# A hybrid RWKV-7 and delta-net layer on one core: scans of two head pairs in one list of steps, decays from running sums read in rows, overlapped inversions, spread modulation sums

## The chip, the cores and the metric

The kernel runs on one core of one Trainium2 chip. The metric is the time of one execution on the device, in microseconds (us), as the median of three runs. A profile of one execution tells where the time goes; its engines are PE (TensorE matmul), PEld (TensorE's weight loads), DVE (VectorE), ACT (ScalarE), POOL (GpSimd) and SP (SyncE, which here only issues DMAs).

## What is computed

One layer over 256 latent tokens and 256 context tokens, 2048 channels, all in float32. The tokens are normalised and modulated, projected once, and go through two token mixers; these are merged, and a feed-forward block follows. Cut to what matters here:

```python
h  = modulate(rmsnorm(x, norm1_w), sh1, sc1)         # x (1, 256, 2048); hc the same of ctx
rw, cv, z, ab, gt = split(h @ w_in, IN_SPLITS)       # and of hc
# RWKV-7: 16 heads of 64, both directions, context first, its final state starts the latents
def step(s, inp):
    r_t, w_t, k_t, v_t, kk_t, b_t = inp
    sa = einsum('bhij,bhj->bhi', s, kk_t)
    s = s * w_t[:, :, None, :] - sa[..., None] * b_t[:, :, None, :] + v_t[..., None] * k_t[:, :, None, :]
    return s, einsum('bhij,bhj->bhi', s, r_t)
# gated delta-net: 8 heads of 128, both directions, chunked
gc    = cumsum(chunks(g), axis=-1)
diff  = gc[..., :, None] - gc[..., None, :]
decay = where(incl, exp(where(incl, diff, 0.0)), 0.0)
lmat  = where(strict, einsum('nbhik,nbhjk->nbhij', kb, kc) * decay, 0.0)
sol   = triangular_solve(lmat, rhs, lower=True, unit_diagonal=True)
q_dec, k_tail, g_last = qc * exp(gc), kc * exp(gc[-1:] - gc), exp(gc[-1])
# merge, output projection, then
x = x + gt1 * y
x = x + gt2 * swiglu(modulate(rmsnorm(x, norm2_w), sh2, sc2), w_gate_up, w_down)
return rmsnorm(x, final_norm_w)
```

## The kernel before

Three stages follow each other. The first makes the modulation of the first norm and the low-rank columns of the projection. The second, some 1125 us long, is written with a planner of its own and is where the change lies. The third runs the merge, the output projection and the feed-forward block as a plain stream of large matmuls.

Every large product is split: a weight `w` is cast to a rounded high part (`whi`, on ACT) and a rest (`wlo`, on DVE), the activations likewise (`hxh`, `hxl`), and three matmuls `hxh,whi`, `hxl,whi`, `hxh,wlo` are added up (line 145 in the second stage, since each operation is recorded through one helper; lines 370 to 372 in the others). A product of 16 weight tiles is thus 48 matmuls of 128x512 (context and latents) or 128x256 (latents alone).

In the second stage each part of the work is a generator that yields operations: `prepare(p)`, `grams(p, d)`, `inverse(p)`, `values(p)`, `scan(p)` for the eight RWKV head pairs p, and `features(h)`, `tokens(h)`, `decays(h)`, `head_grams(h)`, `head_inverse(h)`, `head_scan(h)` for the eight delta-net heads h; `products()` makes all projections, of which 40 gate columns ("g") can be made at nearly any time; `ada_rest()` sums up modulation columns on DVE. The class `Weave` holds a clock for each engine and repeatedly takes the operation that could start first, with the rank of its generator as the tie-break. Its estimates are the numbers of `LAT`: `hop` for the way from one engine to another, `own` for the way to the next operation on the same engine, `turn` for a switch of PE between tile shapes, `grp` for the most matmuls that are issued before it chooses again. It runs when the program is built; what it leaves is a fixed order of instructions for each engine, which then waits on semaphores alone. A generator can also wait for a name that another one has declared ready ("scan", p).

The parts that the change touches:

- `scan(p)` runs the two directions of one pair through eight steps, four over the context (n < 4) and four over the latents. A step is a chain: four small matmuls into a PSUM bank (`s<-VX,LAc` or `s<-VX,LAl`), a copy on ACT (`R`), four matmuls with the inverse (`s<-R,Tx`), two copies on ACT (`VX`), four matmuls with the keys (`s<-VX,KB`), two multiplications on DVE (`VX<-s,et`). Pair p waits for pair p-1.
- `decays(h)` makes for each direction the matrix exp(gc_i - gc_j). It multiplies a triangle of ones by the gates on DVE (`gm`), sums over the tokens in between by a 128x512 float32 matmul with the constant `aft`, takes the exponential on ACT, and masks the result on POOL. A second float32 matmul, 128x256 with `ones`, gives the exponent for the queries (`Qe`).
- `invert(...)` inverts the triangular blocks. Its substitution works on 16x16 blocks that go through DRAM (`scr`, `tscr`) on SP's queue; `head_inverse(h)` starts when that of head h-1 is complete.
- `ada_rest()` loads 64 tiles of 128x1024 on POOL's queue and adds each, times a scalar, to a sum on DVE (`aw<-aw,ck`, two instructions a tile). It starts when the RWKV part is done and goes on as fast as its buffers allow.

Of the kernel before, what the change touches and what calls it, by code (L numbers as in the profile page):

```python
# [11 lines left out]
F32 = mybir.dt.float32  # L12
# [6 lines left out]
P = 128  # L19
D = 2048  # L20
KT = D // P
T = 256
# [7 lines left out]
LAT = dict(dma=2.4, hop=0.3, own=0.1, grp=32, crank=-1, cg=4, turn=0.13)  # L30
# [7 lines left out]
for _name, _w in (("ident", 128), ("ones", 128), ("bd64", 128), ("rmask", 256),  # L38
                  ("low16", 2), ("eye16", 32), ("tri", 256), ("aft", 256), ("q4", 4), ("q2", 2),
                  ("eps", 1), ("gneps", 1)):  # L40
    _C[_name] = (_n, _n + _w)
    _n += _w
# [12 lines left out]
def const_array():  # L55
# [19 lines left out]
    put("aft", np.concatenate([u > v, u < v], 1))  # L75
# [195 lines left out]
def emit(ctx: ExitStack, tc, A, out, dbg=None):  # L271
# [37 lines left out]
    aft = c_("aft").rearrange("p (d t) -> p d t", d=2)  # L309
# [219 lines left out]
    def shift(ps, M, j, dst, ctx_part=True):  # L529

        n = 512 if ctx_part else T
# [11 lines left out]
        if ctx_part:  # L543
            yield add(dst[:M, T + 1:512], ps[:M, T:511], mc[:M, j, 0:1])
            yield add(dst[:M, T:511], ps[:M, T + 1:512], mc[:M, j, 1:2])
# [10 lines left out]
    def invert(pool, Lt, parts, nu, which, full, fill):  # L556
# [11 lines left out]
        Tx = pool.tile([P, nu, 64], F32, tag="ivx", name="Tx", bufs=2)  # L568
# [25 lines left out]
        yield dq(blocks(tl, nb), TT[:nb], 2)  # L594
        for h in range(2):
# [16 lines left out]
        Qm = xt[:, :16 * nu].rearrange("p (u c) -> p u c", c=16)  # L612
# [39 lines left out]
        if full:  # L652
# [3 lines left out]
            for h in range(2):  # L656
# [9 lines left out]
    gtok = cst.tile([P, 4, 16], F32, name="gtok")  # L666
    btok = cst.tile([P, 4, 16], F32, name="btok")
# [8 lines left out]
    arena = arp.tile([P, 9544], F32, name="arena")  # L676
    rplaces = (("k", 512, 1), ("r", T, 1), ("t1", 512, 1), ("kd0", 512, 1), ("kd1", 512, 1), ("kkn", 512, 1), ("sg", 512, 1),
               ("ic", 512, 2), ("ei", 520, 1), ("LT", 1024, 2), ("XT", 512, 1), ("prod", 64, 1),
               ("ivo", 256, 1), ("iv0", 1024, 1), ("v", 512, 1), ("gt", T, 1))
# [11 lines left out]
    def turn(src, g0, ng, put):  # L691
# [3 lines left out]
        for j in range(2):  # L695
            yield [put(j, i, ps[half[i], 0:P * ng].rearrange("p (g k) -> p g k", k=P)[:, :, 64 * j:64 * j + 64])
                   for i in range(2)]
        weave.release(pab)
# [19 lines left out]
    def lowrank():  # L718

        yield s.preload_act_table_set(SIGM)  # L720
        lin = rs.tile([P, 2, 8, 2, 64], F32, tag="KB", name="lin", bufs=2).rearrange("p a b c d -> p (a b c d)")[:96].rearrange("p (j t) -> p j t", j=4)
        raw = rs.tile([P, 4, 64], F32, tag="Y", name="raw").rearrange("p a b -> p (a b)")[:64]
        ab = rs.tile([P, 512], F32, tag="XT", name="ab")[:32]
        for j, b in ((0, pib), (2, psb), (1, mmb), (3, psb)):
            ps = low[j]
            yield from shift(ps, 96, 24 + j, lin[:, j])
            if j < 2:
                yield s.activation(lin[:, j], lin[:, j], AF.Tanh)
# [1009 lines left out]
```

## Time and profile before

| | |
|---|---|
| median of three runs | 2303.02 us (2301.46 to 2306.44) |
| the profiled execution, its own time | 2301.12 us |
| its span, first to last instruction | 2299.2 us |
| mean granted clock of TensorE | 0.98 |
| DVE busy | 1562.2 us (68%) |
| ACT busy | 1058.1 us (46%) |
| POOL busy | 109.7 us (5%) |
| moved by DMA | 430.76 MB, mean 187 GB/s |

Busy time is the time in which at least one instruction of the engine is on its way. Matmuls are pipelined, one starts long before the one in front of it has ended, and their ends are modelled; so what a matmul costs is better read from the distance of two starts than from its own length. A float32 matmul of the small kind leaves two records each. The second stage lasts from about 195 us to 1320 us in this execution.

### The profile page before, as it was taken

The numbers are of one execution on the slowest core, as the hardware profiler recorded it, in microseconds if no ns is written. First come the engines' busy times: TensorE is split into PE (matmuls) and PEld (weight loads), VectorE is DVE, ScalarE is ACT, GpSimd is POOL, SyncE is SP. The second block draws the span as 40 slices with busy tenths as digits, with TensorE's granted clock in tenths as the row PEclk, the third lists the DMA queues.
The fourth block names the chain that finished last, engine by engine and source line by source line (L and its number), as shares of the span: only waits on it lengthen the run. The fifth ranks groups of instructions, "written<-read, shape, count | busy, mean of one in ns | idle before, by whom it ended". The sixth has DMA issues, their size and how long they took to land.

```text
span 2299.2 us, 54667 instructions
## 1 busy us (share of the span) xinstructions
PE 2197.8 (96%) x22904; PEld 1932.8 (84%) x22904; DVE 1562.2 (68%) x3225; ACT 1058.1 (46%) x1922; POOL 109.7 (5%) x185
## 2 busy tenths in 40 slices
PE   7998999999999999999899979899999999999998
PEld 4766677777777787887689979899999999999997
DVE  3446588888877589999777668774666565444544
ACT  3245544544455554454344445444444444444443
POOL 0000000000000011111000031000000000000000
PEclk9998999999999999999899989999999999999999
DMA  9956543443444267666335597863777776566665
GB/s 385 397 149 173 178 116 89 119 108 100 102 100 100 86 212 220 209 203 199 105 85 174 160 346 241 292 224 128 234 236 235 239 235 211 190 185 188 190 188 162
DMA packets 231926, 430.76 MB, mean 187 GB/s; under 512 B 114944, under 2 KB 129152, under 8 KB 227328
## 3 DMA queue, kind: packets, MB, share of 16 engines
q1 hardware_dynamic: 203744, 350.72, 49.6%
q0 software_dynamic: 14112, 51.39, 7.0%
q10 hardware_dynamic: 13824, 25.17, 3.3%
q8 instruction: 179, 2.93, 0.5%
q14 instruction: 67, 0.55, 0.1%
HBM read 401.44 MB, written 25.77 MB: 186 GB/s over the span
## 4 chain that ended last, share of the span: by engine, by line
PE 59%; DVE 9%; DMA 4%; ACT 3%; issue 2%; SPq 1%; POOL 0%; DVEq 0%; ACTq 0%; POOLq 0%
PE mm L145 14%; PE mm L372 12%; PE mm L370 12%; PE mm L371 12%; PE s L145 4%; DVE arena L145 3%; PE pa L145 3%; DVE wlo L145 2%; PE pi L145 1%; DMA wr<-wgu 1%; DVE aw L145 1%; ACT arena L145 1%; DMA aw<-ada_rest 1%; DMA wraw<-pa 1%; DVE wlo L361 1%
## 5 line engine op out<-in xcount | busy, mean ns | idle before, releaser
L361 DVE TENSOR_TENSOR wlo<-wraw,whi 128x1024 fp32r<-128x1024 f32 x328 | 393.9, 1201 | 336.4 <-ACT whi L360 333.1
L360 ACT CAST whi<-wraw 128x1024 fp32r<-128x1024 f32 x328 | 337.4, 1029 | 477.2 <-PE mm L371 437.0
L145 PE MATMUL mm<-hxh,whi 128*128 128x256 f32 (+1 forms) x1376 | 468.1, 340 | 4.7 <-ACT whi L145 4.3
L145 PE MATMUL mm<-hxh,wlo 128*128 128x256 f32 (+1 forms) x1376 | 466.5, 339 | 5.9 <-DVE wlo L145 5.5
L145 PE MATMUL mm<-hxl,whi 128*128 128x256 f32 (+1 forms) x1376 | 465.1, 338 | 0.0
L372 PE MATMUL mm<-hfh,wlo 128*128 128x256 f32 x1344 | 375.5, 279 | 0.0
L370 PE MATMUL mm<-hfh,whi 128*128 128x256 f32 x1344 | 375.4, 279 | 0.0
L371 PE MATMUL mm<-hfl,whi 128*128 128x256 f32 x1344 | 375.2, 279 | 0.0
L145 PEld LDWEIGHTS mm<-hxh,wlo 128*128 128x128 f32 x1376 | 263.4, 191 | 35.9 <-DVE wlo L145 9.2
L145 PEld LDWEIGHTS mm<-hxh,whi 128*128 128x128 f32 x1376 | 263.6, 192 | 32.6 <-issue 6.1
L145 PEld LDWEIGHTS mm<-hxl,whi 128*128 128x128 f32 x1376 | 263.6, 192 | 26.4 <-issue 6.9
L145 DVE TENSOR_TENSOR wlo<-wraw,whi 128x512 fp32r<-128x512 f32 x344 | 236.8, 691 | 59.8 <-ACT whi L145 58.6
L145 ACT CAST whi<-wraw 128x512 fp32r<-128x512 f32 x344 | 205.0, 617 | 106.9 <-PE mm L145 80.7
L372 PEld LDWEIGHTS mm<-hfh,wlo 128*128 128x128 f32 x1344 | 252.9, 188 | 0.4 <-DVE wlo L361 0.4
L370 PEld LDWEIGHTS mm<-hfh,whi 128*128 128x128 f32 x1344 | 253.1, 188 | 0.0
L371 PEld LDWEIGHTS mm<-hfl,whi 128*128 128x128 f32 x1344 | 252.9, 188 | 0.0
L145 DVE TENSOR_TENSOR arena<-arena 128x512 f32<-128x512 f32 (+12 forms) x538 | 133.6, 250 | 22.5 <-DMA arena<-scr 10.1
L370 PE MATMUL mm<-za,whi 128*128 128x256 f32 x512 | 143.0, 279 | 0.0
L372 PE MATMUL mm<-za,wlo 128*128 128x256 f32 x512 | 142.9, 279 | 0.0
L371 PE MATMUL mm<-za,whi 128*128 128x256 f32 x512 | 142.9, 279 | 0.0
L370 PEld LDWEIGHTS mm<-za,whi 128*128 128x128 f32 x512 | 96.4, 188 | 0.0
L371 PEld LDWEIGHTS mm<-za,whi 128*128 128x128 f32 x512 | 96.4, 188 | 0.0
(318 smaller groups left out, 3922.7 us busy)
## 6 DMA issues: line engine op xcount, KB each, us to landing
wraw<-w SPq DMA_DIRECT2D x172, 512.0 KB, 4.0
wraw<-wgu SPq DMA_DIRECT2D x168, 512.0 KB, 4.5
aw<-ada_rest POOLq DMA_DIRECT2D x96, 512.0 KB, 5.0
aw<-ada_first SPq DMA_DIRECT2D x32, 1024.0 KB, 11.0
wraw<-wdn SPq DMA_DIRECT2D x64, 448.0 KB, 3.6
wraw<-wout SPq DMA_DIRECT2D x32, 512.0 KB, 4.7
aw<-ada_gt ACTq DMA_DIRECT2D x64, 256.0 KB, 4.8
wraw<-wdn SPq DMA_DIRECT2D x32, 512.0 KB, 3.6
```

The costliest lines, as they stand in the source:

```text
L145: return Op(self, cost, lambda: getattr(self.engine, name)(out, *a, **k), kind)
L360: S.copy(hi[:, c, :M], raw[:, c, :M])
L361: V.tensor_sub(lo[:, c, :M], raw[:, c, :M], hi[:, c, :M].bitcast(F32))
L370: E.matmul(ps, hi, Xh[:, k, :n], start=first and i == 0, stop=False)
L371: E.matmul(ps, hi, Xl[:, k, :n], start=False, stop=False)
L372: E.matmul(ps, lo, Xh[:, k, :n], start=False, stop=last and i == len(wt) - 1)
```

## The change

- `scan(p)` becomes a scan over "units": unit p runs the four latent steps of pair p and the four context steps of pair p+1 in the same list, step by step, for p from -1 to 7. Each of the four links of a step then carries both pairs: eight matmuls where there were four, one copy `R` of 128x256 instead of 128x128, four copies `VX` instead of two. Units 0 to 6 hold both, unit -1 only context and unit 7 only latents: 9 units of 4 steps, where there were 8 pairs of 8. A step takes both PSUM banks of its pool at once. Matmuls on which no link waits are put behind those on which one does, and the planner's clock is set back by their cost.
- The buffers are cut in two for it: the keys `KB` into a latent and a context part (`KBl`, `KBc`, with twice as many ACT copies of half the size), the values `v` likewise, `LAc` has two buffers instead of three.
- `decays(h)` uses no matmul. `begin()` makes the running sums of all heads once by two scans on DVE and writes them to DRAM (`cumd`). For each head and direction a DMA on SP's queue reads four rows back into all partitions (256 KB), four DVE instructions of 128x128 add the token's own sum and cut at zero, and ACT takes the exponential; the exponent for the queries is taken from the same rows. POOL's mask stays. `egc`, `eta` and `egl` come from the running sums too.
- `head_inverse(h)` waits only until the block transfers of head h-1 are done ("blocks", h-1), and for its end later ("inv", h-1).
- `ada_rest()` lets eight tiles go for each head scan that has ended; its sum has a buffer of its own.
- `LAT`: `hop` 0.3 to 0.225, `own` 0.1 to 0.134, `grp` 32 to 16, `turn` 0.13 to 0.104.

The core of the diff:

```diff
-LAT = dict(dma=2.4, hop=0.3, own=0.1, grp=32, crank=-1, cg=4, turn=0.13)
+LAT = dict(dma=2.4, hop=0.225, own=0.134, grp=16, crank=-1, cg=4, turn=0.104)
...
     def invert(...):
         yield dq(blocks(tl, nb), TT[:nb], 2)
+        yield from free
...
+        weave.ready("blocks", key)
         yield w + late
         yield v.transpose(Tx[:, us[0]], T0[:, us[0]])
         yield v.transpose(T0[:, us[1]], Tx[:, us[1]])
+        yield from after
...
     def scan(p):
+        for m in range(4):
             cm = (m, 3 - m)
             both = slice(m, 8 - m, 7 - 2 * m)
+            sides = []
+            if a:
+                sides.append((4 + m, pr[p], pr[p]["VX"][1], [pr[p]["la", d] for d in range(2)], cm, 0, 0))
+            if b:
+                sides.append((m, pr[p + 1], pr[p + 1]["VX"][0], [pr[p + 1]["lc", d] for d in range(2)], tuple(c + 4 for c in cm), P, T))
+            ps, acc = yield psb, psb
...
+            for n, o, vx, la, cs_, c, st in sides:
+                for d, j, h in dh:
+                    w = slice(0, P) if n else half[1 - j]
+                    ops.append(e.matmul(ps[h, c + 64 * d:c + 64 * d + 64], la[d][w, cm[d], j, 0:64], vx[w, 4 * d + cm[d], j, :],
+                                        start=True, stop=True))
+            late = len(ops)
...
+            yield ops
+            yield -sum((o.cost for o in ops[late:]), 0.0)
+            R1 = rs.tile([P, 4, 64], F32, tag="R1", name="R1")
+            lo, hi = sides[0][5], sides[-1][5] + P
+            yield s.copy(R1.rearrange("p d t -> p (d t)")[:, lo:hi], ps[:, lo:hi])
...
     def begin():
+        yield v.tensor_tensor_scan(t0, ones, sp, 0.0, ALU.mult, ALU.add)
+        yield v.tensor_tensor_scan(t1[:, ::-1], ones, sp[:, ::-1], 0.0, ALU.mult, ALU.add)
+        for d, t in enumerate((t0, t1)):
+            dq(cumd[d], t)
...
     def decays(h):
-            gm = gs.tile([P, 4, P], F32, tag="gm", name="gm")
-            yield v.tensor_mul(gm, tri[:, d].unsqueeze(1).to_broadcast([P, 4, P]),
-                               gtok[:, :, col:col + 1].to_broadcast([P, 4, P]))
-            gf = gm.rearrange("p b c -> p (b c)")
-            ps = yield pab
-            yield e.matmul(ps, aft[:, d], gf, start=True, stop=True)
             ed = gs.tile([P, 4, P], F32, tag=f"Ed{d}", name="Ed")
-            yield s.activation(ed.rearrange("p b c -> p (b c)"), ps, AF.Exp)
-            weave.release(pab)
+            a = cumd[d][0:1]
+            yield dq(ed, bass.AP(a.tensor, a.offset + col * P, [[0, P], [32 * P, 4], [1, P]]))
+            Ed.append(ed)
+        for d, ed in enumerate(Ed):
+            eq = gs.tile([P, T], F32, tag=f"eq{d}", name="eq")
+            yield s.activation(eq, ed[:, 0:2].rearrange("p b c -> p (b c)"), AF.Exp)
+            for b in range(4):
+                yield v.tensor_scalar(ed[:, b], ed[:, b], gtok[:, b, 8 * d + h:8 * d + h + 1], 0.0, ALU.add, ALU.min)
+            yield s.activation(ed, ed, AF.Exp)
             yield g.tensor_mul(ed, ed, tri[:, d].unsqueeze(1).to_broadcast([P, 4, P]))
...
-            ps = yield pab
-            yield e.matmul(ps[:, :T], ones, gf[:, 0:T], start=True, stop=True)
-            eq = gs.tile([P, T], F32, tag="eq", name="eq")
-            yield s.activation(eq, ps[:, :T], AF.Exp)
-            weave.release(pab)
             yield v.tensor_mul(o["Qe"][:, d], o["q"], eq)
...
     def head_inverse(h):
         if h:
-            yield "inv", h - 1
+            yield "blocks", h - 1
...
     def ada_rest():
         for i in range(4 * KT):
             if i > 2:
                 yield "added", i - 3
+            if i % 8 == 0 and i:
+                yield "gscan", i // 8 - 1
             weave.add(500, row_tile(i))
```

What the planner makes of it stands in the order of the built program. The first place is PE inside an RWKV scan. Before, one latent step of a pair; `s<-VX,LAl` is its first link, `s<-R,Tx` its second, `pa<-arena,C` and `mm<-...` are other work in between:

```order
L145 MATMUL s<-VX,LAl 64x64 x4
L145 MATMUL pa<-arena,C 128x512
L145 MATMUL s<-R_7984,Tx 64x64 x4
L145 MATMUL s<-VX,C 64x128 x2
L145 MATMUL s<-LAl,VX 64x64 x4
L145 MATMUL mm<-hxl,whi 128x512
```

In the changed program, the step that carries two pairs (`LAl` of the one, `LAc` of the other):

```order
L144 MATMUL s<-VX,LAl 64x64 x4
L144 MATMUL s<-VX,LAc 64x64 x4
L144 MATMUL s<-LAl,VX 64x64 x4
L144 MATMUL mm<-hxl,whi 128x256
L144 MATMUL mm<-hxh,wlo 128x256
L144 MATMUL mm<-hxh,whi 128x256
L144 MATMUL s<-R_6988,Tx 64x64 x8
L144 MATMUL s<-VX,C 64x128 x4
```

The context step of the next pair stands in the same stay at the small tiles as the latent step, and the output's part `s<-LAl,VX` has moved ahead of `R`. Counted over the whole second stage, PE leaves the large products for other work 461 times before (255 times for matmuls on a part of the array, 206 for whole-array float32 matmuls) and 371 times in the changed program (190 and 181).

The second place is DVE and SP around a head's decays. Before, on DVE (`arena<-C,gtok` is `gm`):

```order
L145 SCALAR_TENSOR_TENSOR Y<-pa,Y 128x256
L145 STREAM_TRANSPOSE Tx<-arena 128x512
L145 TENSOR_TENSOR arena<-C,gtok 128x512
L145 STREAM_TRANSPOSE arena<-Tx 128x512
L145 TENSOR_TENSOR wlo<-wraw,whi 128x512
```

In the changed program on DVE (`arena<-arena,gtok` is the sum and cut), and on SP (`arena<-cumd` is the read of the rows):

```order
L144 TENSOR_SCALAR arena<-arena,gtok 128x128
L144 SCALAR_TENSOR_TENSOR arena<-mm,PR,arena 128x2x255
L144 TENSOR_SCALAR arena<-arena,gtok 128x128
L144 TENSOR_TENSOR wlo<-wraw,whi 128x512
L144 TENSOR_SCALAR arena<-arena,gtok 128x128
```

```order
L155 DMA wraw<-w 128x1024
L155 DMA scr_105<-LT 64x4x64
L155 DMA arena<-cumd 128x4x128
L155 DMA scr_105<-T_10335 64x4x64 x2
L155 DMA scr_105<-LT 64x4x64
L155 DMA arena<-cumd 128x4x128
L155 DMA arena<-scr_105 64x16x16
L155 DMA wraw<-w 128x1024 x2
```

One long instruction has become four short ones (three are shown) with other work between them, and a read of rows stands in SP's queue between the transfers of an inversion and ahead of weights.

The third place is POOL's queue, where the masks of the decays (`TENSOR_TENSOR arena<-arena,C`) and the loads of the modulation sums take turns. Before, after the first masks:

```order
L123 DMA aw<-ada_rest 128x1024 x3
L145 TENSOR_TENSOR arena<-arena,C 128x512
L123 DMA aw<-ada_rest 128x1024 x8
L145 TENSOR_TENSOR arena<-arena,C 128x512
L123 DMA aw<-ada_rest 128x1024 x5
```

In the changed program:

```order
L122 DMA aw<-ada_rest 128x1024 x6
L144 TENSOR_TENSOR arena<-arena,C 128x512
L122 DMA aw<-ada_rest 128x1024 x2
L144 TENSOR_TENSOR arena<-arena,C 128x512
L122 DMA aw<-ada_rest 128x1024 x3
```

The loads, 64 in both, stand in 14 stretches of the queue instead of 10, and the last of them behind the last mask, where five masks followed the loads before.

More of the change, by code (lines that the diff above doesn't have):

```diff
@@ new lines, in scan @@
+            late = len(ops)
+            for n, o, vx, la, cs_, c, st in sides:
+                if 0 < n < 7:
+                    for j, h in enumerate(half):
+                        ops.append(e.matmul(c3(acc[h, st:st + P]), ident[h, h], vx[h, both, j, :], start=first(j), stop=False))
+            yield ops
+            yield -sum((o.cost for o in ops[late:]), 0.0)
+            for n, o, vx, la, cs_, c, st in sides:
+                for j, h in enumerate(half):
+                    yield s.copy(vx[h, both, j, :], c3(ps[h, T + c:T + c + P]))
@@ L1129, in emit @@
     gorder = ([2, 3, 0, 1], [3, 2, 1, 0])
-    TF = []
+    TF, vts = [], []
     def begin():
@@ L1479, in emit @@
             weave.add(10 * p, scan(p))
+        weave.add(0, scan(-1))
         weave.add(100, begin())
```

230 lines of the change are left out of this document (124 added, 106 removed).

## The prediction

> **What bounds the kernel now.** I read the head of the page first, then the busy time by stages (start:end of the stage, its length, busy time of each engine with instructions, granted clock of PE, DMA share, GB/s).
>
> ```profile
> span 2299.2 us, 54667 instructions
> 195.00:740.00 545.00, 525.35 (x7446) 397.80 (x7444) 433.26 (x1096) 273.83 (x666) 16.59 (x47) 0.97 0.45 116
> 740.00:1000.00 260.00, 252.95 (x2655) 206.54 (x2653) 211.09 (x501) 129.96 (x260) 31.77 (x49) 1.00 0.59 179
> 1000.00:1200.00 200.00, 186.05 (x1847) 152.58 (x1833) 168.62 (x430) 91.69 (x178) 21.35 (x32) 0.96 0.51 151
> 1200.00:1320.00 120.00, 118.20 (x1418) 113.76 (x1419) 78.72 (x220) 56.02 (x123) 1.34 (x2) 1.00 0.54 159
> 1380.00:2299.20 919.20, 896.28 (x7579) 890.50 (x7577) 541.43 (x720) 401.73 (x513) 13.32 (x21) 0.99 0.67 211
> ```
>
> The change lies in 195 to 1320 us: RWKV pairs to 740, delta-net heads behind. PE is busy for 525.35, 252.95, 186.05 and 118.20 of these 1125 us, so it idles 42.5 us in all. DVE comes second (433 of 545, 380 of 460), and ACT and DMA have half their time free. The stage therefore ends when PE has done its work, and a part of the change is worth what it takes from PE: work, time lost between pieces of work, waits. What lies outside the stage is the same code, and I leave its 1174 us as they are. Which waits PE has left is told by the waits of PE in the stage (total, times, longest):
>
> ```profile
> PE pa L145 <- ACT arena L145: 6.0, 9, 0.9
> PE pi L145 <- DVE arena L145: 5.3, 7, 2.2
> PE pa L145 <- DVE arena L145: 4.0, 7, 1.4
> PE mm L145 <- DVE wlo L145: 2.0, 3, 0.9
> ```
>
> They are short and scattered: no single wait decides, since other work stands ready in PE's order nearly always.
>
> **The decays' matmuls.** The change takes 16 float32 matmuls of 128x512 (`aft`) and 16 of 128x256 (`ones`) from PE. The groups of PE show them together with the sums of squares, which stay (records, two a matmul; busy, mean ns of a record; idle before):
>
> ```profile
> L145 PE MATMUL pa<-arena,C 128*128 128x512 f32 x64 | 37.4, 668 | 10.7 <-ACT arena L145 6.9 <-DVE arena L145 3.8
> L145 PE MATMUL pa<-arena,C 128*128 128x256 f32 x48 | 15.0, 395 | 1.8 <-ACT arena L145 1.2 <-DVE kta L145 0.6
> ```
>
> Records overlap, so I price by starts in the timeline of PE (start, length):
>
> ```profile
> 1028.23 1.13 PE L145 MATMUL pa<-arena,C 128*128 128x512 f32 x2 [0.91 <-ACT arena L145]
> 1028.79 0.79 PE L145 MATMUL mm<-hxh,whi 128*128 128x512 f32 x1
> 1029.42 0.39 PE L145 MATMUL mm<-hxl,whi 128*128 128x512 f32 x1
> 1029.65 0.39 PE L145 MATMUL mm<-hxh,wlo 128*128 128x512 f32 x1
> ...
> 1034.02 0.59 PE L145 MATMUL pa<-arena,C 128*128 128x256 f32 x2
> 1034.44 0.38 PE L145 MATMUL s<-gvt,TF 128*128 128x128 f32 x2
> ```
>
> From 1028.23 to 1029.42 there is one such matmul and one product of 512 columns, which takes 0.23 (1029.42 to 1029.65): 0.96 us. The 256-column one takes 0.42. So 16 x 0.96 + 16 x 0.42 = 22.1 us. Bounds: twice the mean length, 16 x (1.34 + 0.79) = 34.1 us above; below, two records at the products' spacing of 0.23 and half of it, 16 x (0.46 + 0.23) = 11.0 us. I take 22.1, since starts are measured and ends modelled. The two transposes of the running sums that `begin` gains and the four small matmuls that it drops happen once and cancel within a microsecond.
>
> **Fewer stays at small work.** Each time PE leaves the products for something else, and when it returns, it loses time. A context step of the scan shows it:
>
> ```profile
> 583.90 0.40 PE L145 MATMUL mm<-hxh,whi 128*128 128x512 f32 x1
> 584.13 0.39 PE L145 MATMUL mm<-hxl,whi 128*128 128x512 f32 x1
> 584.45 0.45 PE L145 MATMUL s<-VX,LAc 128*64 128x64 f32 x8
> 584.84 0.50 PE L145 MATMUL mm<-hxh,wlo 128*128 128x512 f32 x1
> 585.17 0.39 PE L145 MATMUL mm<-hxh,whi 128*128 128x512 f32 x1
> 585.41 0.40 PE L145 MATMUL mm<-hxl,whi 128*128 128x512 f32 x1
> 585.73 0.45 PE L145 MATMUL s<-R,Tx 64*64 64x64 f32 x8
> ```
>
> Products stand 0.23 apart; the last before the stay takes 0.32 (584.13 to 584.45) and the first behind it 0.33 (584.84 to 585.17), so a stay costs 0.09 + 0.10 = 0.19 us beside its own matmuls, whose number the change leaves as it is. The order has 65 fewer stays at parts of the array (255 to 190): 12.4 us. It has 25 fewer at whole-array float32 work, where only the way back seems to cost, about 0.09: 2.2 us. Together 14.6 us; bounds 0 (if a stay of twice the length loses twice as much) and 90 x 0.19 = 17.1 us. I take 14.6, since the loss is seen at the two ends of a stay and not inside it.
>
> The planner's smaller `hop` puts dependent work earlier on PE. In the step above, `R` on ACT ended 0.45 us before `s<-R,Tx` began, so there is room, and the two-pair step gives its longer copy more work to hide behind:
>
> ```profile
> 585.01 0.27 ACT L145 COPY R<-s 128x128 f32<-128x128 f32 x1 [1.95 <-PE s L145]
> ```
>
> I cost the new constants at nothing; if the cover is gone, each of the 36 steps could wait 0.1 to 0.3 us at three places, 11 to 32 us, which the range holds.
>
> **DVE, ACT, POOL, SP.** On DVE the 16 `gm` go and 64 short sums come:
>
> ```profile
> L145 DVE TENSOR_TENSOR arena<-C,gtok 128x512 f32<-128x512 f32 x16 | 10.8, 677 | 0.0
> L145 DVE TENSOR_SCALAR arena<-arena 128x128 f32<-128x128 f32 x3 | 0.7, 220 | 0.0
> L145 DVE TENSOR_SCALAR arena<-arena,al 128x128 f32<-128x128 f32 x1 | 0.3, 279 | 0.0
> L145 DVE SCALAR_TENSOR_TENSOR aw<-aw,ck 128x512 f32<-128x512 f32 x120 | 89.1, 752 | 3.7 <-DMA aw<-ada_rest 3.5
> ```
>
> 64 x 0.22 to 0.28 is 14 to 18 us, so DVE gains 3 to 7 us of work, behind PE. What matters more is the last row: 89 us of modulation sums, which the change stretches from the heads' first part over all of them. The stages say where this helps: PE idles 21.0 us of the 460 from 740 to 1200 (4.6%), where these sums are made, and 1.8 of the 120 behind (1.5%), where they are done. At 1.5% throughout it would be 14 us less; a part of the sums now falls into the last 120 us, so I take 6 us. The other end is a loss of 12 us, DVE's and ACT's waits above (6.0, 5.3 and 4.0) coming back for most of their length once more.
>
> ACT's copies of the keys double in number at half the size; four-fold `VX` and wider `R` add little:
>
> ```profile
> L145 ACT COPY KB<-pa 64x256 f32<-64x256 f32 x128 | 46.9, 366 | 14.4 <-PE pa L145 12.6
> L145 ACT COPY VX<-s 64x128 f32<-64x128 f32 x128 | 33.2, 259 | 51.0 <-PE s L145 49.3
> ```
>
> 256 x 0.259 = 66.3 us against 46.9, 19 us more on an engine that has 271 of 545 us free in that stage: nothing, as long as PE bounds. Overlapped inversions take no instruction away; they free the planner's hand, and with PE filled they are worth nothing by themselves.
>
> **The sum.** 2299.2 - 22.1 - 14.6 - 6 = 2256.5 us of span. The profiled execution took 1.9 us more than its span, and the median of the runs is another 1.9 above it, so the forecast is 2260 us, 43 below 2303.02. All bounds together: 34.1 + 17.1 + 14 = 65 us gained (2238), or 11.0 + 0 - 12 = 1 us lost (2304).
>
> **Rivals.** *The rows come late* (slower). A head's reads wait on SP for the grams of the head before, with transfers of the inversion and weights queued behind them, and its decays then need the landing, an exponential, four sums, an exponential and POOL's mask, in place of one matmul and one exponential. The nearest loads, KB each and median us to landing, and the longest wait for such a transfer:
>
> ```profile
> arena<-sgd__1342 SPq DMA_DIRECT2D x28, 256.0 KB, 3.5
> scr<-arena SPq DMA_DIRECT2D x32, 128.0 KB, 2.7
> DVE arena L145 <- DMA arena<-scr: 10.1, 3, 7.5
> ```
>
> For it speaks that PE takes its order as it stands: a late matrix stops `LT`, and so the inversion's matmuls. Against it: 3.5 us is close to the 2.4 us and the transfer that the planner counts, and heads overlap. It decides from 43/8 = 5.4 us a head; at 8 us a head, about the longest wait of 7.5 us, it would cost 64 us: 2324.
>
> *DVE and POOL block each other* (little gain). The trace shows a sum on DVE beside POOL's mask:
>
> ```profile
> 1060.54 2.24 DVE L145 SCALAR_TENSOR_TENSOR aw<-aw,ck 128x512 f32<-128x512 f32 x2
> 1061.12 1.11 POOL L145 TENSOR_TENSOR arena<-arena,C 128x512 f32<-128x512 f32 x1 [1.77 <-ACT arena L145]
> ```
>
> Two sums took 2.24 instead of 1.50 us (752 each). The new short sums of the second direction stand where the mask of the first runs; if each of the 16 masks held DVE for its 1.11 us, that is 17.8 us, and if DVE then set the heads' end, the 6 us were lost too: 2260 + 17.8 + 6 = 2284. Against it: DVE has a sixth of its time free there, and the masks are as many as before. The Trainium skill, "SBUF — State Buffer", section "SBUF: two separate sides", says that the port pair shared by VectorE and GpSimd is an exclusive lock held for a whole instruction; by that rule this loss is real on DVE, and the rows above agree with it.
>
> *Stays cost as before* (it does not do what it says): the fuller stays lose inside what they save at their ends, 14.6 us given back: 2275.
>
> *More*: the waits shrink in all of the stage, to 0.5%: 37 us for my 6, 2229.
>
> **How the numbers follow.** Forecast, within 2240 to 2275: 0.62. More: 0.07. Stays: 0.10. DVE and POOL: 0.07. No change: 0.03. Late rows or another loss that large: 0.11. A measurement of this kernel tells 0.2%, 4.6 us, from no change. Faster is 0.62 + 0.07 + 0.10 + 0.07 = 0.86, the same 0.03, slower 0.11. The range reaches from the lower bound of the sum, 2238, to 2298, where the known terms are nearly all given back; what is left out is 0.05 below and 0.14 above.
>
> **What would show it.** Right: the second stage ends near 1277 us, `aft`'s 32 records of 128x512 are gone, products beside a stay still take 0.32 and 0.33, PE idles below 42.5 us in the stage, and the modulation sums reach to its end. Wrong: waits of PE's `pi` or `pa` groups on DVE or on the reads of `cumd` that total over 30 us; a stage in which DVE is busier than PE; more PE idle time among the two-pair steps; or a later end of the third stage than 979 us behind the second.

## The result, and the profile after

The changed kernel takes 2327.5 us in the median (2317.66 to 2331.92, 7 runs), the kernel before 2304.28 us on the same chip (2300.26 to 2307.48, 7 runs): a ratio of 1.0097, 95% interval 1.0076 to 1.0119. It is 1% slower, where 2260 us had been forecast.

The head of the page and the busy time by stages of the changed kernel (columns as in the prediction). The second stage is taken to the last matmul of the heads, which now ends at about 1347 us:

```profile
span 2330.1 us, 54687 instructions
195.00:740.00 545.00, 513.62 (x7437) 409.40 (x7436) 431.36 (x1054) 278.64 (x770) 16.04 (x47) 0.96 0.46 123
740.00:1000.00 260.00, 234.41 (x2417) 189.64 (x2415) 189.90 (x515) 125.01 (x259) 22.60 (x31) 0.95 0.45 135
1000.00:1200.00 200.00, 175.06 (x1898) 145.43 (x1896) 165.53 (x447) 85.21 (x171) 21.68 (x32) 0.92 0.52 151
1200.00:1347.00 147.00, 137.22 (x1538) 130.19 (x1537) 114.30 (x295) 68.84 (x144) 13.69 (x23) 0.97 0.70 219
```

In the kernel before, the last matmul of the heads ends at 1326 us, 6 us behind the 1320 of the prediction. The whole stage before, to this mark:

```profile
195.00:1326.00 1131.00, 1087.77 (x13381) 875.46 (x13380) 896.51 (x2257) 554.97 (x1237) 73.18 (x133) 0.98 0.50 142
```

PE is now busy for 513.62 + 234.41 + 175.06 + 137.22 = 1060.3 us of 1152, before for 1087.8 of 1131. Its busy time fell by 27.5 us. Its idle time rose from 43.2 to 91.7 us, by 48.5. So the stage is 21 us longer, and the third stage, whose code is the same, takes 2330.1 - 1347 = 983 us against 973. The question is where the idle time comes from. The matmuls that the change removes are gone; the groups of PE in the changed kernel's second stage, to be read beside the x64 and x48 of before:

```profile
L144 PE MATMUL pa<-arena,C 128*128 128x512 f32 x30 | 17.3, 661 | 5.3 <-ACT arena L144 5.3
...
L144 PE MATMUL pa<-arena,C 128*128 128x256 f32 x16 | 4.8, 379 | 0.0
```

The waits of PE in the changed kernel's second stage (total, times, longest) have long single ones; before, none was over 2.2 us:

```profile
PE pi L144 <- issue: 14.3, 7, 6.9
PE s L144 <- DVE Vn L144: 8.3, 11, 3.4
PE s L144 <- DVE St L144: 8.1, 2, 7.8
```

The pauses that end on nothing the profile shows (`issue`) were short before:

```profile
PE pi L145 <- issue: 2.9, 7, 1.1
```

They are taken up in the last section. Behind the others stand two kinds of transfer. The waits of ACT and of DVE in that stage:

```profile
ACT arena L144 <- DMA arena<-cumd: 21.2, 6, 7.5
...
DVE acc L144 <- DMA aw<-ada_rest: 19.5, 5, 8.8
```

and the DMA issues of the whole execution (KB each, median us from issue to landing):

```profile
arena<-cumd SPq DMA_DIRECT2D x16, 256.0 KB, 10.2
...
scr<-T SPq DMA_DIRECT2D x16, 64.0 KB, 9.9
```

The row reads land 10.2 us after their issue; a load of the same size from `sgd` took 3.5 us before. DVE's waits for modulation loads were 3.5 us in all before. The pause of 7.8 us shows how the two hang together. In the timeline of the changed kernel (start, length, idle time before and what ended it):

```profile
1074.83 1.16 SPq L155 DMA_DIRECT2D arena<-cumd  x1
...
1076.65 0.48 SPq L155 DMA_DIRECT2D arena<-cumd  x1
...
1077.27 0.53 POOL L122 DMA_DIRECT2D aw<-ada_rest  x1 [3.14 <-DVE T L144]
...
1091.01 0.75 DVE L144 SCALAR_TENSOR_TENSOR acc<-aw,ck,acc 128x512 f32<-128x512 f32 x1 [8.76 <-DMA aw<-ada_rest]
1091.68 0.28 DVE L144 COPY St<-s 128x128 f32<-128x128 f32 x1
...
1092.02 0.80 PE L144 MATMUL s<-St,arena 128*128 128x128 f32 x2 [7.77 <-DVE St L144]
```

Two row reads start; a modulation load that starts 0.6 us behind them is late; DVE, which takes its instructions in order, stands at the sum that needs it for 8.76 us; the copy `St` of a head's scan is next in line, and PE waits 7.77 us for that copy.

A pause of PE can cost more than its own length. Around the end of this one PE's granted clock is half for 10 us (columns as above):

```profile
1087.00:1097.00 10.00, 4.98 (x23) 4.99 (x24) 5.75 (x16) 1.14 (x2) 0.00 (x0) 0.50 0.50 150
1097.00:1107.00 10.00, 10.00 (x69) 9.16 (x68) 8.69 (x25) 2.57 (x6) 1.94 (x2) 0.99 0.54 175
```

Up to 1097 us products of 256 columns start 0.21 us apart, behind it 0.12. The trace has 18 such stretches of half clock in the stage, 109 us in all, and PE idles for at least 1.3 us in the 8 us ahead of each; before there are 8, 44 us in all. An estimate from these stretches, half of PE's busy time in them, is 47 us lost against 20. With it taken off, PE's busy time fell by some 55 us, and not by 27.5.

### The profile page after: what moved, and what is told of

Same layout as the page of the kernel before. It is cut to its first block, busy times and chain, and to the rows that moved or that the text cites. A ratio compares the mean times of both kernels' runs of the same rounds, so it can differ in the third digit from the quotient of the medians.

```text
span 2330.1 us, 54687 instructions
## 1 busy us (share of the span) xinstructions
PE 2174.0 (93%) x22834; PEld 1936.1 (83%) x22834; DVE 1566.4 (67%) x3277; ACT 1062.3 (46%) x2031; POOL 109.8 (5%) x185
## 4 chain that ended last, share of the span: by engine, by line
PE 42%; DMA 7%; DVE 4%; issue 3%; ACT 2%; SPq 0%; POOL 0%; DVEq 0%; ACTq 0%; POOLq 0%
PE mm L370 12%; PE mm L369 11%; PE mm L368 11%; PE mm L144 5%; PE s L144 2%; DMA wr<-wgu 2%; DVE wlo L359 1%; DMA wraw<-wgu 1%; DMA aw<-ada_rest 1%; ACT whi L358 1%; DMA wraw<-pa 1%; PE pa L144 1%; PE pi L144 1%; DVE arena L144 1%; DVE acc L144 0%
## 5 line engine op out<-in xcount | busy, mean ns | idle before, releaser
L144 DVE TENSOR_TENSOR arena<-arena 128x512 f32<-128x512 f32 (+12 forms) x538 | 132.7, 249 | 24.1 <-DMA arena<-scr 10.3
L144 ACT ACTIVATE arena<-arena 128x512 f32<-128x512 f32 (+4 forms) x132 | 76.9, 593 | 88.2 <-DVE arena L144 51.7
L144 DVE SCALAR_TENSOR_TENSOR acc<-aw,ck,acc 128x512 f32<-128x512 f32 x120 | 89.3, 750 | 19.8 <-DMA aw<-ada_rest 19.5
```

The lines of the kernel that those rows point to most:

```text
L144: return Op(self, cost, lambda: getattr(self.engine, name)(out, *a, **k), kind)
```

## Was it the row reads?

*packed_rows* keeps the order of all engines as it is and stores the running sums so that the four pieces of one head and direction lie together:

```diff
-    cumd = dpool.tile([2, P, P], F32, name="cumd")
+    cumd = dpool.tile([2, 32, 4 * P], F32, name="cumd")
-            dq(cumd[d], t)
+            dq(bass.AP(cumd[d].tensor, cumd[d].offset, [[P, 4], [4 * P, 32], [1, P]]), t)
-            yield dq(ed, bass.AP(a.tensor, a.offset + col * P, [[0, P], [32 * P, 4], [1, P]]))
+            yield dq(ed.rearrange("p b c -> p (b c)"), bass.AP(a.tensor, a.offset + col * 4 * P, [[0, P], [1, 4 * P]]))
```

> The changed kernel, with the running sums stored so that the four pieces of one head and direction lie together: each row read brings 2 KB to a partition in one piece where it brought four pieces of 512 B. Everything else, the order on every engine too, is as in the changed kernel (2327 us). Theory 'late rows' (the 16 row reads land after 10.2 us in the median, and loads beside them take twice as long: weights 9.8 for 4.2 us, modulation loads 9.8 for 4.9, turned blocks 10.3 for 4.9): the reads land in under 6 us, the loads beside them fall back towards 4 to 5 us, PE's idle time of the delta-net part (800 to 1342 us, about 52 us) falls by 20 to 30, and the time to 2297 to 2307. Theories 'short constants' (the planner's new wait constants make pauses) and 'spread sums' (modulation sums stand in the way of the heads): the time stays within 6 us of 2327 whatever the reads do.

2294.26 us, ratio 0.9953 (0.9930 to 0.9976): 33 us faster than the changed kernel, and 0.5% faster than the kernel before. Its stages, then its waits of ACT and DVE, then its issues:

```profile
195.00:740.00 545.00, 516.97 (x7437) 411.26 (x7437) 431.39 (x1054) 280.43 (x773) 15.31 (x47) 0.95 0.45 122
740.00:1000.00 260.00, 240.30 (x2644) 192.58 (x2647) 203.34 (x547) 126.67 (x265) 24.02 (x33) 0.97 0.48 144
1000.00:1200.00 200.00, 185.94 (x1899) 158.04 (x1892) 177.60 (x493) 100.85 (x197) 25.15 (x35) 0.97 0.57 171
1200.00:1311.00 111.00, 106.88 (x1316) 102.25 (x1315) 87.22 (x216) 50.16 (x111) 10.42 (x18) 0.98 0.73 235
```

```profile
ACT arena L144 <- DMA arena<-cumd: 3.7, 2, 3.4
...
DVE acc L144 <- DMA aw<-ada_rest: 6.9, 5, 2.5
```

```profile
arena<-cumd SPq DMA_DIRECT2D x16, 256.0 KB, 5.5
...
scr<-T SPq DMA_DIRECT2D x16, 64.0 KB, 5.2
```

The stage now ends at 1311 us. PE's busy time is 1050.1 us, its idle time 65.9: of the 91.7 us 26 are gone, 22 of them behind 740 us, where the rows are read. The 10 us of busy time that are gone too belong to the same instructions: the half clock fell from 109 to 82 us, by the same estimate from 47 to 38 us lost. The reads became quicker, and so did what runs beside them. Here are the issues of the same place in both orders, 1074 to 1080 us in the changed kernel:

```profile
aw<-ada_rest POOLq DMA_DIRECT2D x3, 512.0 KB, 12.8
arena<-cumd SPq DMA_DIRECT2D x2, 256.0 KB, 12.3
wraw<-w SPq DMA_DIRECT2D x1, 512.0 KB, 10.2
...
scr<-T SPq DMA_DIRECT2D x1, 64.0 KB, 15.6
```

and 1053 to 1058 us in packed_rows:

```profile
aw<-ada_rest POOLq DMA_DIRECT2D x2, 512.0 KB, 6.2
arena<-cumd SPq DMA_DIRECT2D x2, 256.0 KB, 6.3
wraw<-w SPq DMA_DIRECT2D x1, 512.0 KB, 5.8
...
scr<-T SPq DMA_DIRECT2D x1, 64.0 KB, 8.7
```

A modulation load beside slow reads lands after 12.8 us, beside quick ones after 6.2; the turned blocks of the inversion (`scr<-T`, queued behind the reads on SP) after 15.6 and 8.7.

*padded_rows* asks what makes the reads slow. It leaves them in four pieces of 512 bytes for each partition, and only moves the pieces from 16 KB apart to 16.5 KB:

```diff
-    cumd = dpool.tile([2, P, P], F32, name="cumd")
+    cumd = dpool.tile([2, 4 * 33, P], F32, name="cumd")
-            dq(cumd[d], t)
+            dq(bass.AP(cumd[d].tensor, cumd[d].offset, [[33 * P, 4], [P, 32], [1, P]]), t)
-... [[0, P], [32 * P, 4], [1, P]]))
+... [[0, P], [33 * P, 4], [1, P]]))
```

> The changed kernel with its reads of four 512-byte pieces for each partition, but with the pieces 16.5 KB apart in memory in place of 16 KB. Order as in the changed kernel. If the reads are slow by the number of pieces (512 a read): landing stays at 9 to 11 us and the time at 2320 to 2332. If it is the 16 KB distance of the pieces: landing falls under 7 us and the time under 2310.

2295.15 us, ratio 0.9968 (0.9950 to 0.9986). Its waits and issues, in the same columns:

```profile
ACT arena L144 <- DMA arena<-cumd: 3.8, 1, 3.8
...
DVE acc L144 <- DMA aw<-ada_rest: 9.3, 5, 3.1
```

```profile
arena<-cumd SPq DMA_DIRECT2D x16, 256.0 KB, 6.1
...
scr<-T SPq DMA_DIRECT2D x16, 64.0 KB, 5.1
```

The reads have as many pieces as in the changed kernel, but land after 6.1 us instead of 10.2, and the kernel is as fast as with one piece of 2 KB, within the intervals. So it is the distance of 16 KB that costs, not the number of pieces. Since the order is the same in all three kernels, this is shown: the place of the rows in memory costs 1.3 to 1.4%.

Two kernels let the reads slow and told the planner of it. *told_slow* gives them 7.3 us of the load queue, *told_late* lets only the reader wait 7 us longer:

```diff
-            yield dq(ed, bass.AP(...))
+            yield dq(ed, bass.AP(...), 10)
```

```diff
-            yield dq(ed, bass.AP(...))
+            yield dq(ed, bass.AP(...)) + 7.0
```

> The changed kernel with the planner told that a row read takes 10 us (7.3 us of queue and 2.4 of landing, where it reckoned 0.7 and 2.4); the reads themselves are as slow as they were. Theory 'late rows': the work that needs the rows is dealt later and less waits in line for them (ACT's 21.2 us of waits for the rows fall under 8), but the loads beside the reads stay slow: the time falls by part of the loss, to 2308 to 2322. Theories 'short constants' and 'spread sums': within 8 us of 2327.

> The changed kernel with its slow row reads; the planner is told only that the rows land 7 us later, and keeps its books of the load queue as they were. If the price of the slow reads is work that stands in line for the rows (ScalarE waits 21.2 us for them): most of the 33 us comes back, 2298 to 2308. If it is the loads beside them that come late (weights, modulation loads, turned blocks, PE's instructions): no more than a third comes back, 2316 to 2330.

2366.41 us (1.0280, 1.0246 to 1.0313) and 2343.48 us (1.0187, 1.0152 to 1.0222): both slower than the changed kernel, which neither theory had said. A truer estimate did not make a better order. A likely reason is taken up two sections below: every such edit deals the whole order anew.

## The other parts of the change, taken out or made alone

*sums_unspread* and *before_sums_spread* take the spreading of the modulation sums out of the changed kernel and put it alone into the kernel before:

```diff
             if i > 2:
                 yield "added", i - 3
-            if i % 8 == 0 and i:
-                yield "gscan", i // 8 - 1
```

> The changed kernel without the wait that spreads the modulation sums over the heads (they may run as soon as their buffers allow, as before). Theory 'spread sums': VectorE's 19.5 us of waits for these loads go, PE's pauses of 7.8 and 4.3 us behind them too, and the time falls by 10 to 20 us to 2307 to 2317. Theory 'late rows': the same loads now meet the row reads of the first heads only; the time stays within 8 us of 2327 or falls by less than 10. Theory 'short constants': no change within 8 us.

> The kernel before with one part of the change alone: the modulation sums spread over the heads (eight row tiles wait for each head's scan). Term c as predicted (some 6 us, bounds 14 gain and 12 loss) and as its removal from the changed kernel showed (11 us slower without it): 2289 to 2298. If spreading helps only beside slow row reads: within 4 us of 2303.

Without it the changed kernel takes 2338.39 us (1.0147, 1.0106 to 1.0188), 0.5% more; with it alone the kernel before takes 2294.86 us (0.9966, 0.9940 to 0.9993). Both say a gain, of about 8 to 11 us, but both orders are dealt anew, and the next section shows that this alone can move the time by more. The expectation that spreading was the trouble fell.

*decays_by_matmul* makes the decays of the changed kernel on PE again; *before_packed_rows* gives the kernel before the row decays alone, packed:

```diff
+            yield v.tensor_mul(ed, tri[:, d]..., gtok[:, :, col:col + 1]...)
+            yield e.matmul(ps[:, :T], ones, gf[:, 0:T], start=True, stop=True)
+            yield s.activation(eq, ps[:, :T], AF.Exp)
...
+            yield e.matmul(ps, aft[d], gf, start=True, stop=True)
+            yield s.activation(gf, ps, AF.Exp)
-            yield dq(ed, bass.AP(...))
```

> The changed kernel with the decays made on TensorE again, as before the change (two matmuls for each head and direction, through PSUM banks, and no row reads at all); the rest of the change stays. 'Late rows' with term a as predicted (the matmuls cost PE 22.1 us, bounds 11.0 to 34.1): 22 us over the kernel with packed rows (2294), so about 2316, and below the changed kernel (2327), since slow rows cost 33 and save 22. If the matmuls had been nearly hidden (under 11 us): at or below 2305. If the loss of the change had another cause than the rows: at or above 2327.

> The kernel before with this one part of the change: decays from running sums read in rows, stored so that a read brings 2 KB in one piece. Scans, constants, inversions and modulation sums stay as before. Term a as predicted: 22 us less PE work and no more waiting, 2304 to about 2282 (2270 to 2293 by its bounds). If rows cost as much in waits as they save: 2299 to 2309. The two-pair part (300 to 800 us) has PE idle 12 us as before.

2293.67 us (0.9969, 0.9947 to 0.9991) and 2302.53 us (1.0001, 0.9987 to 1.0016). In both places taking 32 large float32 matmuls from PE moved nothing, where 22 us had been expected. The row of the delta-net part shows how, first of the kernel before, then of before_packed_rows:

```profile
800.00:1326.00 526.00, 503.09 (x5146) 433.63 (x5146) 433.89 (x1100) 247.54 (x500) 55.50 (x85) 0.98 0.58 173
```

```profile
800.00:1329.00 529.00, 492.84 (x5102) 431.27 (x5103) 433.34 (x1141) 248.51 (x500) 59.33 (x87) 0.96 0.62 185
```

PE's busy time in the delta-net part fell by 10.3 us, its idle time rose from 22.9 to 36.2, by 13.3. The granted clock fell as well, from 0.98 to 0.96. What it lacks times the length is an estimate of 526 x 0.02 = 10.5 us lost before and 529 x 0.04 = 21.2 in before_packed_rows; at one clock PE's work thus fell by some 21 us, as foretold, and idle time and lower clock took them back. The waits of PE there, in before_packed_rows, are the heads' own chains (the three took 1.1, 1.7 and 1.3 us before):

```profile
PE s L145 <- DVE Vn L145: 4.9, 5, 1.3
PE pi L145 <- DVE T L145: 4.6, 3, 2.6
...
PE pi L145 <- ACT T L145: 3.2, 1, 3.2
```

So PE seems to reach the next matmul of an inversion or a scan earlier, and to wait there for DVE or ACT.

*packed_inversions_apart* lets a head's inversion begin only when the one before it has ended; *packed_unpaired* (with the constants of before) runs the two pairs' halves in steps of their own:

```diff
-            yield "blocks", h - 1
+            yield "inv", h - 1
```

```diff
-        for m in range(4):
+        for m, a, b in [(m, q, not q) for m in range(4) for q in (True, False) if both_sides[0 if q else 1]]:
```

> The kernel with packed rows, but a head's inversion begins only when the inversion of the head before it has ended, as in the kernel before. Theory 'chain' (in the delta-net part the heads' chains of inversions and scans set the pace, not PE's work: taking 22 us of PE work out of it moved nothing): the overlap is worth something and its loss makes 2300 to 2315. If PE's work sets the pace there: within 6 us of 2294.

> The kernel with packed rows and the old constants (2287 on its chip, ratio 0.9948), in which a scan step takes one pair at a time again: the context half and the latent half of two neighbouring pairs stand in one list of units, but each in steps of its own (422 stays at small work for 370). Term b as predicted (a stay costs 0.19 us beside its work, 14.6 us in all, bounds 0 to 17.1): 0.4 to 0.7% slower, ratio 0.999 to 1.002. If pairing gave back what it saved (PE pauses for instructions and longer copies between steps: PE idles 25 us in the two-pair part, 12 before): ratio 0.991 to 0.997.

2308.93 us (1.0041, 1.0025 to 1.0057), 0.9% above packed_rows, and 2339.8 us (1.0172, 1.0154 to 1.0190), 2.2% above packed_old_constants. Both parts gain as tried, the pairing more than all of the predicted term b. How much of it belongs to them is limited by what follows.

## How far a new deal alone moves the time

Each edit above but the two of `cumd` also deals the order of the second stage anew. Seven kernels change no work at all, only constants or the tie-break of the planner: *old_constants*, *packed_old_constants*, *before_new_constants* exchange the line

```diff
-LAT = dict(dma=2.4, hop=0.225, own=0.134, grp=16, crank=-1, cg=4, turn=0.104)
+LAT = dict(dma=2.4, hop=0.3, own=0.1, grp=32, crank=-1, cg=4, turn=0.13)
```

(before_new_constants the other way); *packed_hop* and *before_hop* move `hop` alone, 0.225 to 0.23 and 0.3 to 0.29; *packed_breaks* prefers products after 64 small matmuls in a row, and *packed_breaks_old* does so with the old constants:

```diff
+                    wait = 0.4 if lane is self.tensor and self.small >= 64 and isinstance(w[5][0].kind, tuple) else 0.0
-                    key = (max(self.free.get(lane, 0.0), at), w[0])
+                    key = (max(self.free.get(lane, 0.0), at) + wait, w[0])
```

> The changed kernel with the planner's four constants of before (hop 0.3, own 0.1, grp 32, turn 0.13). Theory 'short constants': PE's idle time in the two-pair part (300 to 800 us, 31.8 us, 12.2 before) falls back by 10 to 15 us and the time to about 2305 to 2315. Theory 'late rows': the delta-net part keeps its pauses; time within 8 us of 2327, either way, since every order is dealt anew.

> The kernel with packed rows and the planner's four constants of before. If the new constants cost the two-pair scans what they cost the kernel before (2345 for 2303 there): 2285 or less. If they suit the new scans, as the prediction had it in costing them at nothing: within 8 us of 2294; above 2302 they are a part of the gain.

> The kernel before with the planner's new constants alone. As the prediction had it (costed at nothing): within 6 us of 2304, fewer stays at small work (437 runs of it for 460, some 4 us). Theory 'short constants' (work is now dealt before its data are there): 2312 or more, with PE idle over 20 us in the two-pair part (12.2 before).

> Packed rows with one constant of the planner moved by 2% (hop 0.23 for 0.225): no work and no wait is added or taken away, the order is only dealt anew. If a new deal alone moves the time little, it stays within 5 us of 2294 (ratio 0.993 to 0.998). If deals differ by as much as packed_breaks_old did (23 us above the same kernel without the breaks): 8 us or more off, either way; then single re-dealt kernels can't carry a claim of 10 us.

> The kernel before with hop 0.29 for 0.3 and nothing else: a new deal of the old work. If that moves little: within 5 us of 2303. If the kernel before stands at a good deal among its neighbours (new constants alone made it 42 us slower): 8 us or more slower, and part of the gain that the prediction expected was already in that deal.

> The kernel with packed rows, and one rule more in the planner: after 64 small matmuls in a row it prefers a product group that can start within 0.4 us. Theory 'fetch' (PE runs out of instructions in dense small work: its 16 KB fetches follow each other no faster than every 3.3 to 3.5 us, and it resumes 1.2 to 1.5 us after one has ended; such pauses take 11.1 us of the two-pair part here, 3.9 before): they fall under 6 us and the time by 3 to 8 us, to 2286 to 2291. Rival: the density over several microseconds stays the same, only places change; 2291 to 2300, the pauses stay near 11 us.

> Packed rows, the old constants and the break after 64 small matmuls together. If the break's gain (2286.9 for 2294.3) was one of fetches: ratio 0.990 to 0.993. If it was only another deal of the order: 0.993 to 0.997, as without the break.

| kernel | median, us | ratio to the kernel before (95%) |
|---|---|---|
| old_constants | 2321.62 | 1.0080 (1.0052 to 1.0109) |
| packed_old_constants | 2287.21 | 0.9948 (0.9931 to 0.9966) |
| before_new_constants | 2344.91 | 1.0185 (1.0152 to 1.0218) |
| packed_hop | 2299.49 | 0.9980 (0.9962 to 0.9998) |
| before_hop | 2354.12 | 1.0219 (1.0202 to 1.0235) |
| packed_breaks | 2286.92 | 0.9926 (0.9900 to 0.9953) |
| packed_breaks_old | 2310.56 | 1.0038 (1.0020 to 1.0057) |

Moving `hop` by 0.01 us makes the kernel before 51 us slower. By stages, before_hop:

```profile
195.00:740.00 545.00, 520.74 (x7388) 398.31 (x7387) 426.88 (x1043) 271.28 (x654) 18.00 (x47) 0.98 0.46 120
740.00:1000.00 260.00, 237.62 (x2348) 183.00 (x2351) 192.85 (x462) 120.61 (x246) 30.59 (x44) 0.95 0.52 157
1000.00:1200.00 200.00, 168.06 (x1611) 133.06 (x1612) 157.61 (x411) 78.57 (x155) 22.67 (x35) 0.91 0.48 139
1200.00:1373.00 173.00, 170.73 (x1991) 159.45 (x1989) 119.74 (x335) 79.73 (x171) 4.85 (x6) 1.00 0.50 149
```

The same work, but PE idles for 1178 - 1097.2 = 81 us where it idled for 43.2. The 43.2 us were thus not a property of the old kernel's work but of one deal of it. Around packed_rows the deals lie closer, from 0.9926 to 1.0038. The break's gain of 7 us in one deal is a loss of 23 us in another, so the theory that it saves instruction fetches has no support from the times: PE's pauses that end 1.05 to 1.6 us after an instruction packet, counted from the trace's packets in the two-pair part (300 to 800 us), fell only from 11.1 to 8.8 us there, and rose from 7.3 to 14.5 with the old constants.

*one_read* is packed_breaks_old with both directions of a head in one read of 4 KB for each partition:

```diff
-    cumd = dpool.tile([2, 32, 4 * P], F32, name="cumd")
+    cumd = dpool.tile([48, 2, 4 * P], F32, name="cumd")
...
+        yield dq(both.rearrange("p d b c -> p (d b c)"), bass.AP(a.tensor, a.offset, [[0, P], [1, 8 * P]]))
```

> As packed_breaks_old, and both directions' rows of a head come in one read of 4 KB for each partition, where two reads of 2 KB followed each other. 'Late rows' says that the second direction still lost time behind the first (5.5 us to landing each, the second issued 0.5 to 2.6 us behind): 0 to 10 us less than packed_breaks_old, 2275 to 2288. If rows are no longer late: within 5 us of it.

2306.47 us (1.0028, 1.0015 to 1.0040): within 5 us of packed_breaks_old, so no further gain from the reads is seen once they land in 5 to 6 us; this order, too, is dealt anew.

## Why the prediction was wrong

**The rows (the step that failed most clearly).** The prediction priced the reads by "the nearest loads", 3.5 us for 256 KB, called that close to what the planner counts, and gave *the rows come late* 0.11, deciding from 5.4 us a head. They land after 10.2 us, and this rival is what happened: 33 us, or 4.1 us a head, shown by two kernels of the same order. Its time of 2324 us was close by luck: it put 64 us for the rows on top of 2260, where the rows cost 33 and the rest came from the next step. Its way was right only in part: ACT's waits for the rows are 21.2 us, but the loads beside them, to which the prediction gave no cost of their own, came late too and held DVE (19.5 us), and PE's instructions once.

**"The stage ends when PE has done its work" (the step behind the rest).** With the rows mended the kernel takes 2294 us, still 34 above the forecast. Terms a and b as work taken from PE were not too large: its busy time went from 1087.8 to 1050.1 us in packed_rows, 37.7 us for the 36.7 foretold, and by some 55 with the estimate for half clock taken off. What was wrong was to count this as time, with idle time staying at 42.5 less 6, and no cost for the clock. Idle time went to 65.9, and the half clock behind pauses from an estimated 20 us to 38. PE was nearly always busy because this one deal of the order fitted, and a share of 96% busy was read as a bound of PE. A bound would not move by 51 us with a constant that changes no work.

**Term a**, 22.1 us: the matmuls went, and no time with them, in the old kernel or the new. Of the 13.3 us of idle time that came in their place, 8.6 stand in the three waits of the heads' chains shown above. The two kernels are new deals, and one deal can hide 22 us (before_hop hides more); that both hide it is less likely, but not excluded.

**Term b**, 14.6 us: pairing gains, 2.2% as tried, but in an order dealt anew. The ends of a stay cost what was foretold: in the changed kernel the last product before one takes 0.20 us (581.74 to 581.94) and the first behind it 0.22 (582.84 to 583.06), where such products stand 0.12 apart. What the pairing is worth in time stays open.

**Term c**, 6 us: as tried right in sign and near in size, 8 us alone and 11 in the changed kernel. Both are less than a new deal alone can move, so the term is not shown.

**The planner's constants at nothing**: right for the new scans (0.9948 for 0.9953, and 1.0080 for 1.0097, the intervals overlap). In the old kernel they cost 42 us, but a change of `hop` by 0.01 cost 51.

**Overlapped inversions** "worth nothing by themselves": 0.9% as tried, 15 us, in an order dealt anew. That the heads' chains and not work decide there would explain it, but is not shown.

**DVE and POOL block each other**: DVE's busy time is 1566.4 us against 1562.2, 4 us more, inside the 3 to 7 that the short sums were to bring. In the trace of the changed kernel none of the 64 short sums, 273 ns each in the mean, runs beside a mask, so the loss that this rival priced is not seen. **The third stage**, taken as unchanged, is 983 us for 973 by the same mark, and 981 in packed_rows; why is open.

Of the signs that the prediction named for being wrong, more PE idle time among the two-pair steps came (31.4 us for 19.7 from 195 to 740), and a later end of the third stage. The waits of `pi` and `pa` groups on DVE, which were to total over 30 us, come to 14.7, and PE waits for no read of `cumd` itself. The loss came through `s` groups that wait on DVE, DVE and ACT that wait on loads, and pauses by `issue`, which no sign named.

What stays open: why 16 KB is a bad distance, why the truer estimates of the two told kernels dealt worse orders, what makes the third stage longer, and how the gain of pairing splits from its deal. The fastest kernel seen is packed_breaks, 0.74% below the kernel before, but its interval and that of packed_rows overlap.

## What to carry to other kernels

Price a new transfer by its own pieces and their addresses, not by a load of equal size, and look at what will run beside it: here part of the loss came through loads beside the slow reads. Count with a pause of PE the lower clock that can follow it. Where an order of instructions is fixed by a planner, a little idle time on an engine does not make it the bound; move a constant that changes no work, see how far the time swings, and take no smaller range than that. Try causes in kernels that keep the order: of eighteen runs, the two that did so are the ones that show a cause.

## What the runs showed of the hardware

**The distance of pieces in memory.** A read of 256 KB, four pieces of 512 bytes for each of 128 partitions, all partitions the same 2 KB: 10.2 us with the pieces 16 KB apart, 6.1 us with 16.5 KB, 5.5 us in one piece. The Trainium skill, "DMA: Bandwidth & Descriptors", section "Latency and other measured facts", reports a loss in copies whose rows for neighbouring partitions lie a large power of two apart: 207 GB/s at 512 KiB, 164 at 2 MiB, 103 at 4 MiB, cured by padding of 4 KiB and not by 192 bytes. Here a distance of 16 KB, between the pieces of one partition, was enough for a loss, and 512 bytes of padding cured most of it. That the two have one mechanism is not shown.

**Slow reads hold up PE's instructions.** In the changed kernel PE stopped in the middle of a group of small matmuls:

```profile
761.88 0.92 SPq L155 DMA_DIRECT2D arena<-cumd  x2
...
765.19 0.36 PE L144 MATMUL pi<-arena,Tx 32*32 32x16 f32 x20
772.47 1.68 PE L144 MATMUL pi<-arena,Tx 32*32 32x16 f32 x108 [6.91 <-issue]
```

The DMA view of 765.5 to 770.2 us has packets of the ordinary queue alone; that of 770.2 to 771.3 has one instruction packet of 16 KB (queue, kind: packets, MB, share of 16 engines):

```profile
q1 hardware_dynamic: 701, 0.49, 35.9%
```

```profile
...
q8 instruction: 1, 0.02, 5.7%
```

PE goes on at 772.47, about 1.2 us after that packet. In packed_rows, with the same order, the pause at this place is shorter:

```profile
763.59 0.36 PE L144 MATMUL pi<-arena,Tx 32*32 32x16 f32 x20
766.91 1.08 PE L144 MATMUL pi<-arena,Tx 32*32 32x16 f32 x108 [2.96 <-issue]
```

The Trainium skill, "Runtime: NRT & Kernel Launch", section "Instruction fetch mechanics", says that instructions are refilled in blocks of 16 KiB (256 instructions) and that this is mostly hidden. The trace agrees with the size of the block. It is not hidden here: among small matmuls these packets follow each other no faster than every 3.4 us, and the longer pauses by `issue` end 1.2 to 1.5 us behind one. So the reading is that PE runs out of instructions, and that a packet beside slow reads comes late. Pauses that end 1.05 to 1.6 us behind such a packet took 16.5 us of the two-pair part in the changed kernel and 11.1 in packed_rows.
